# A RWKV/conv/Fourier/MoE backbone on one core: GpSimd's elementwise work in the attention units goes to VectorE, a broadcast copy to TensorE

## Chip, cores and metric

One core of a Trainium2 chip runs one program, the whole two-layer block. The metric is the device time of one execution in microseconds (us); the median of three runs of the kernel before is 3627.87 us (3625.42 to 3634.18).

## The reference, cut to what matters

1280 tokens (256 of context, 1024 latent) of width 1024 go through two layers. Each layer projects the normed tokens to 2944 columns; half of the model is a bidirectional RWKV-7 time mixing with 8 heads of 64:

```python
w_log = -softplus(-(decay_w0 + tanh(lw) @ decay_w2)) - 0.5
decay = exp(-exp(w_log))
a = sigmoid(iclr_a0 + la @ iclr_a2)
kk = normalised(k * k_k)
k_dir = k * (1.0 + (a - 1.0) * k_a)
s = s * d_t - (s @ kk_t)(kk_t * a_t)^T + v_t k_t^T
y = sum over directions of s r_t;  bonus = sum(r * k_dirs[dn] * r_k) * v
```

The rest of a layer (a gated short convolution, a Fourier mix, an output projection, a mixture of 32 experts) is not touched by the change.

## The kernel before, in words

The recurrence is computed in chunks of C = 64 tokens, of which there are 20. For each layer the work ahead of the sequential scan is cut into 16 units (L818). A unit is a pair of heads p (head e = 0 on partitions 0 to 63, e = 1 on 64 to 127), a half hf of the tokens (640 tokens, 10 chunks) and a direction d. The units run in pairs that share p and hf. Beside them runs the input projection (L386): 128x512 fp32r matmuls that a pacing object places on TensorE between the matmuls of the units, a fixed share per unit (L838). The program's order of each engine comes from a scheduler with its own timeline of the engines; SyncE (SP) issues nearly all DMAs from one queue in program order.

What one unit does:

- `gates` (L492): two matmul groups make the logits; ScalarE takes tanh of half of them, and VectorE maps each by 0.5x + 0.5 to a sigmoid (L508) for the decays `sg` and for `aa` (the a of the reference). VectorE's prefix scan over `sg` (L510) and two exponentials give E and Ei.
- `heads` (L477), once per pair of units: GpSimd copies the inverse norms `inv` out over 64 columns per head (L480), five matmuls with the identity transpose them (L484), and VectorE multiplies them with k (L485) to the normalised `kk`.
- `factors` (L517): ScalarE makes 1 + (a - 1) k_a from `aa` and VectorE multiplies it with k to `kd` (L523, L524). `aa` is multiplied by Ei (L526). `bk` holds, for each chunk, 128 columns: the keys kd Ei and the beta kk aa. VectorE fills the lower 64 partitions (L534, L535), GpSimd the upper 64 (L532, L533); the two heads have the two blocks in opposite order. VectorE makes `ar` (L536 to L542). In every second unit GpSimd adds the `kd` of the two directions and multiplies the sum with r (L544, L545), and a DMA writes it to prD (L546).
- `attn` (L549): matmuls of `bk` with `ar` (L561), masked by VectorE into X (L566), DMAs of `ar` and X (L573 to L578), then, in two groups, five TensorE transposes of `bk` (L583), copied by ScalarE (L587) and stored (L589).
- `inverse` (L591): for three units at a time GpSimd inverts 120 triangular 32x32 blocks by 60 small operations (L605, L607); ScalarE transposes them and DMAs store them (L612, L622). It reads the blocks that `attn` wrote to gD (L600).
- `merge` (L625): loads the blocks of one unit again (L635, L636) into the single buffer `zt` and makes 64x64 inverses by small matmuls (L645, L647), copied by ScalarE and stored (L655). The merge of unit u - 6 is loaded at unit u.

`bk`, `ar`, `aa` and `kd`'s sum have one buffer (or two for `kd`), so a unit waits for the readers of the one before. The loop that orders it all:

```python
g = gates(p, hf, d, *lw)
if prev is not None:
    attn(*prev)
if u % 2 == 0:
    kk, kds = heads(p, hf, rks[p][1], invs[p]), []
prev = (p, hf, d) + factors(p, hf, d, *rks[p], kk, g, kds)
```

Of the kernel before, what the change touches and what calls it, by code (L numbers as in the profile page):

```python
# [9 lines left out]
F32 = mybir.dt.float32  # L10
# [3 lines left out]
AF = mybir.ActivationFunctionType  # L14
OP = mybir.AluOpType
# [4 lines left out]
P = 128  # L20
# [11 lines left out]
C = 64  # L32
# [15 lines left out]
HT, HC = T // 2, NCH // 2  # L48
# [75 lines left out]
class K:  # L124
# [223 lines left out]
    def inproj(self, l, last):  # L348
        nc, tc, a = self.nc, self.tc, self.a
# [5 lines left out]
        sp = tc.alloc_tile_pool(name="ip", bufs=1, reuse_waits="tile")  # L355
        un = tc.alloc_tile_pool(name="un", bufs=1, side="right", reuse_waits="tile")
# [3 lines left out]
        pace = Pace(tc)  # L360
        om = sp.tile([P, 15], F32, name="om")
        nc.vector.tensor_scalar(om, self.vec("mu", 0, 15), -1.0, 1.0, op0=OP.mult, op1=OP.add)
        oka = sp.tile([P, 4], F32, name="oka")
        nc.vector.tensor_scalar(oka, self.vec("ka", 0, 4), -1.0, 1.0, op0=OP.mult, op1=OP.add)
        wah = sp.tile([P, 2, 8], F32, name="wah")
        nc.vector.tensor_scalar(wah[:, 0], self.vec("w0", 0, 8), 0.5, None, op0=OP.mult)
        nc.vector.tensor_scalar(wah[:, 1], self.vec("a0", 0, 8), 0.5, None, op0=OP.mult)
# [15 lines left out]
        def bank():  # L383
            return bk_[0].tile([P, 1024], F32, name="ps1", bufs=bk_[1])
# [91 lines left out]

        def heads(p, hf, k, inv):  # L477

            kk = un.tile([P, HT], F32, name="kk", bufs=2)
            nc.gpsimd.tensor_copy(kk.rearrange("q (t e d) -> q t e d", e=2, d=64),  # L480
                                 inv[:, 5 * hf:5 * hf + 5, :, None].to_broadcast([P, 5, 2, 64]))
            ps = bank()
            for t in range(5):
                nc.tensor.matmul(ps[:, t * P:(t + 1) * P], kk[:, t * P:(t + 1) * P], self.ident, start=True, stop=True)  # L484
            nc.vector.scalar_tensor_tensor(kk, k[:, hf * HT:(hf + 1) * HT], self.vec("kk", p), ps[:, :HT],  # L485
                                           op0=OP.mult, op1=OP.mult)
            return kk.rearrange("q (c t) -> q c t", t=C)
# [4 lines left out]
        def gates(p, hf, d, lw, la):  # L492


            t0 = hf * HT
            hs = slice(64 * d, 64 * d + 64)
            sg = un.tile([P, HC, C], F32, name="sg")
            aa = un.tile([P, HC, C], F32, name="aa")
            for i, (w, src, dst) in enumerate(((w2, lw, sg), (a2, la, aa))):
                ps = bank().rearrange("q (h t) -> q h t", h=2)[:, :, :320]  # L500
                for q in range(2):
                    mm = nc.tensor.matmul(ps[:, q], w[hs, p * P:(p + 1) * P],
                                          src[hs, t0 + 320 * q:t0 + 320 * (q + 1)], start=True, stop=True)
                pace.point(mm, W_GATE[i])

                nc.scalar.activation(flat(dst).rearrange("q (h t) -> q h t", h=2), ps, AF.Tanh,
                                     bias=wah[:, i, 4 * d + p:4 * d + p + 1], scale=0.5)
                nc.vector.tensor_scalar(dst, dst, 0.5, 0.5, op0=OP.mult, op1=OP.add)  # L508
            rev = slice(None, None, -1) if d else slice(None)
            nc.vector.tensor_tensor_scan(flat(sg)[:, rev], rst, flat(sg)[:, rev], 0.0, op0=OP.mult, op1=OP.add)  # L510
            E = un.tile([P, HC, C], F32, name="E")
            Ei = un.tile([P, HC, C], F32, name="Ei")
            nc.scalar.activation(E, sg, AF.Exp, scale=-CC)
            nc.scalar.activation(Ei, sg, AF.Exp, scale=CC)
            return aa, E, Ei

        def factors(p, hf, d, r, k, kk, g, kds):  # L517
            aa, E, Ei = g
            rev = slice(None, None, -1) if d else slice(None)
            e0 = 0 if d else C - 1  # L520
            nc.vector.tensor_copy(self.wc[d][:, p, hf * HC:(hf + 1) * HC], E[:, :, e0])
            kd = un.tile([P, HC, C], F32, name="kd", bufs=2)
            nc.scalar.activation(kd, aa, AF.Identity, bias=oka[:, p:p + 1], scale=self.vec("ka", p))  # L523
            nc.vector.tensor_tensor(kd, kd, cv(k, hf), op=OP.mult)  # L524
            kds.append(kd)
            nc.vector.tensor_tensor(aa, aa, Ei, op=OP.mult)  # L526


            ar = un.tile([P, 2, HC, C], F32, name="ar")
            bk = un.tile([P, HC, 2, C], F32, name="bk")  # L530
            lo, hi = slice(0, 64), slice(64, 128)
            nc.gpsimd.tensor_tensor(bk[hi, :, 0, :], kd[hi], Ei[hi], op=OP.mult)  # L532
            nc.gpsimd.tensor_tensor(bk[hi, :, 1, :], kk[hi, :, rev], aa[hi, :, rev], op=OP.mult)  # L533
            nc.vector.tensor_tensor(bk[lo, :, 1, :], kd[lo], Ei[lo], op=OP.mult)  # L534
            nc.vector.tensor_tensor(bk[lo, :, 0, :], kk[lo, :, rev], aa[lo, :, rev], op=OP.mult)  # L535
            if d == 0:  # L536
                nc.vector.tensor_tensor(ar[:, 0, :, 1:], kk[:, :, 1:], E[:, :, :C - 1], op=OP.mult)
                nc.vector.tensor_copy(ar[:, 0, :, 0:1], kk[:, :, 0:1])
            else:
                nc.vector.tensor_tensor(ar[:, 0, :, 1:], kk[:, :, C - 2::-1], E[:, :, :0:-1], op=OP.mult)  # L540
                nc.vector.tensor_copy(ar[:, 0, :, 0:1], kk[:, :, C - 1:C])
            nc.vector.tensor_tensor(ar[:, 1], cv(r, hf), E, op=OP.mult)  # L542
            if len(kds) == 2:
                nc.gpsimd.tensor_tensor(kds[0], kds[0], kds[1], op=OP.add)  # L544
                nc.gpsimd.tensor_tensor(kds[0], kds[0], cv(r, hf), op=OP.mult)  # L545
                nc.sync.dma_start(self.prD[p][:, hf * HT:(hf + 1) * HT], flat(kds[0]))  # L546
            return ar, bk

        def attn(p, hf, d, ar, bk):  # L549

            GR = ((0, 5), (5, 5))
            half = lambda e: slice(64 * e, 64 * e + 64)
            img = slice(hf * HC, (hf + 1) * HC)

            Xs = [un.tile([P, 2, HC, C], F32, name="X", bufs=2) for _ in range(2)]
            for c0, n in ((0, 4), (4, 3), (7, 3)):
                ps = bank().rearrange("q (e c s t) -> q e c s t", e=2, s=2, t=C)
                for c in range(n):
                    for e in range(2):
                        h = half(e)  # L560
                        mm = nc.tensor.matmul(ps[:, e, c], bk[h, c0 + c].rearrange("q s t -> q (s t)"), ar[h, :, c0 + c, :],  # L561
                                              start=True, stop=True)
                pace.point(mm, W_ATTN)
                for e in range(2):
                    mv = msk[:, d, e].rearrange("q (s t) -> q s t", s=2)
                    nc.vector.tensor_tensor(Xs[e][:, :, c0:c0 + n].rearrange("q s c t -> q c s t"), ps[:, e, :n],  # L566
                                            mv[:, None].to_broadcast([P, n, 2, C]), op=OP.mult)
            for e in range(2):
                h, o = half(e), half(1 - e)
                X = Xs[e]  # L570
                sn = "q s (n c) t -> q (s n) (c t)"
                for v, rows in ((ar[h], h), (X[o], o)):
                    nc.sync.dma_start(self.rlD[d][e][img, rows, p, :].rearrange("m q x -> q m x"),  # L573
                                      v.rearrange(sn, c=2))
                nc.sync.dma_start(self.abD[d][hf * 5:hf * 5 + 5, h, 1, p, :].rearrange("n q x -> q n x"),
                                  X[h, 1].rearrange("q (n c) t -> q n (c t)", c=2))
                m = (2 * place[p, hf, d] + e) * HC
                nc.sync.dma_start(self.mats(self.gD, m, HC), X[h, 0])  # L578

            for c0, n in GR:  # L580
                ps = bank()
                for c in range(n):
                    mm = nc.tensor.transpose(ps[:, c * P:(c + 1) * P], bk[:, c0 + c].rearrange("q s t -> q (s t)"),  # L583
                                             self.ident)
                pace.point(mm, W_ATTN)
                bt = un.tile([P, 5, P], F32, name="bt", bufs=2)
                nc.scalar.activation(bt[:, :n].rearrange("q c t -> q (c t)"), ps[:, :n * P], AF.Copy)  # L587
                ch = slice(hf * HC + c0, hf * HC + c0 + n)
                nc.sync.dma_start(self.btD[d][ch, :, p, :].rearrange("c q x -> q c x"), bt[:, :n])  # L589

# [1351 lines left out]
```

## Time and profile before

| what | us |
|---|---|
| median of 3 runs (lowest, highest) | 3627.87 (3625.42, 3634.18) |
| the profiled execution | 3623.64 |
| its span, first to last instruction | 3621.7 |
| TensorE busy in the span | 3063.4 |
| VectorE busy | 2281.6 |
| ScalarE busy | 1880.5 |
| GpSimd busy | 1178.0 |

The profiled execution took 3623.64 us, 1.9 us more than its span. The units of the first layer run from about 170 to 600 us of the span, those of the second from about 2000 to 2430 us. Engines are named PE (TensorE matmuls), PEld (its weight loads), DVE (VectorE), ACT (ScalarE), POOL (GpSimd) and SPq (SyncE's queue). A name such as `bk<-kd,Ei` is the tile written and the tiles read; an idle time is put down to what ended it.

### The profile page before, as it was taken

Reading aid. Unit: us, or ns where it says so; the run is one execution under the profiler, and the core shown is the slowest. Engines: PE = TensorE matmul, PEld = TensorE weight load, DVE = VectorE, ACT = ScalarE, POOL = GpSimd, SP = SyncE. Lnnn points to the kernel's source line nnn. Section 1 sums busy time; section 2 is a strip of 40 time slices with the busy share of each in tenths; the row PEclk is TensorE's granted clock in tenths of the full one; section 3 lists DMA queues with packets and bytes.
Section 4 is the critical chain, followed back from the end, with each engine's and each line's share of the span. In section 5 each row is a group of like instructions: output and inputs, shape, how many; then the busy total and the mean of one; then the engine's idle time right before and its main releaser. Section 6 shows DMA issues by size and latency. Waiting matters only on the chain. (4 is left out here: it accounts for less than half of the span.)

```text
span 3621.7 us, 59282 instructions
## 1 busy us (share of the span) xinstructions
PE 3063.4 (85%) x22308; PEld 2426.6 (67%) x22308; DVE 2281.6 (63%) x3543; ACT 1880.5 (52%) x2838; POOL 1178.0 (33%) x1101
## 2 busy tenths in 40 slices
PE   6998788888997999999829988778878978999992
PEld 3776666676686777777616766556666857777772
DVE  4265566134487888888672665652334778888886
ACT  4343433335344777778652434323343467777783
POOL 0037675211221222222140276743113122233323
PEclk8998888899998999999959988778988989999996
DMA  6677888879746899999667578889795488899995
GB/s 241 207 167 173 185 192 181 246 230 315 260 142 243 334 339 338 365 373 363 257 227 258 144 169 181 176 180 252 240 285 167 133 315 317 331 366 364 360 366 205
DMA packets 708060, 922.35 MB, mean 255 GB/s; under 512 B 335074, under 2 KB 561259, under 8 KB 657852
## 3 DMA queue, kind: packets, MB, share of 16 engines
q1 hardware_dynamic: 669456, 871.05, 75.8%
q0 software_dynamic: 38304, 47.49, 3.9%
q8 instruction: 177, 2.90, 0.3%
q14 instruction: 111, 0.91, 0.1%
q10 hardware_dynamic: 12, 0.00, 0.0%
HBM read 726.92 MB, written 203.23 MB: 257 GB/s over the span
## 5 line engine op out<-in xcount | busy, mean ns | idle before, releaser
L176 DVE TENSOR_TENSOR hl<-ld,hl 128x1024 fp32r<-128x1024 f32 x734 | 869.2, 1228 | 54.2 <-ACT hl L175 44.2
L175 ACT ACTIVATE hl<-ld 128x1024 fp32r<-128x1024 f32 x796 | 798.5, 1052 | 38.4 <-PE pR L1571 21.9
L1571 PE MATMUL pR<-hl,wk 128*128 128x512 f32 x1560 | 455.1, 400 | 0.0
L1571 PE MATMUL pU<-hl,wk 128*128 128x512 f32 x1560 | 446.9, 395 | 0.0
L397 PE MATMUL pb<-hh,wh 128*128 128x512 f32 (+1 forms) x1000 | 393.0, 394 | 10.2 <-ACT wh L175 5.4
L397 PE MATMUL pb<-hl,wh 128*128 128x512 f32 (+1 forms) x1000 | 389.1, 390 | 0.0
L397 PE MATMUL pb<-hh,wl 128*128 128x512 f32 (+1 forms) x1000 | 385.4, 386 | 0.0
L1595 PE MATMUL pA<-hl,wk 128*128 128x512 f32 x1560 | 382.9, 401 | 0.5 <-ACT wk L175 0.5
L1571 PEld LDWEIGHTS pU<-hl,wk 128*128 128x128 f32 x1560 | 294.5, 189 | 68.3
L1595 PEld LDWEIGHTS pA<-hl,wk 128*128 128x128 f32 x1560 | 292.7, 191 | 64.0 <-ACT wk L175 0.7
L1571 PEld LDWEIGHTS pR<-hl,wk 128*128 128x128 f32 x1560 | 288.3, 189 | 60.7 <-ACT wk L175 0.3
L176 POOL TENSOR_TENSOR hl<-ld,hl 128x1024 fp32r<-128x1024 f32 x62 | 184.2, 2971 | 422.4 <-ACT hl L175 422.4
L397 PEld LDWEIGHTS pb<-hh,wh 128*128 128x128 f32 x1000 | 200.2, 200 | 76.8 <-issue 14.1
L1602 POOL DMA_INDIRECT yb<-wk,sca x64 | 94.8, 1482 | 468.2 <-ACT wk L1601 452.1
L1276 PE MATMUL pA<-hl,wk 128*128 128x512 f32 x864 | 226.6, 413 | 7.7 <-POOL wk L176 4.0
L397 PEld LDWEIGHTS pb<-hl,wh 128*128 128x128 f32 x1000 | 201.1, 201 | 37.9 <-issue 10.3
L397 PEld LDWEIGHTS pb<-hh,wl 128*128 128x128 f32 x1000 | 200.2, 200 | 35.2 <-issue 4.6
L1100 POOL DMA_DIRECT2D yD<-yt x72 | 58.0, 805 | 433.7 <-ACT yt L1099 391.6
L1276 PEld LDWEIGHTS pA<-hl,wk 128*128 128x128 f32 x864 | 163.0, 195 | 49.2 <-issue 6.0
L1088 DVE TENSOR_TENSOR tm<-pR,ST 128x256 f32<-128x256 f32 x76 | 32.1, 423 | 249.4 <-PE pR L1083 237.4
L175 ACT ACTIVATE wk<-pm 128x256 fp32r<-128x256 f32 (+1 forms) x195 | 88.8, 455 | 185.6 <-PE pm L1586 169.3
L607 POOL TENSOR_TENSOR gt<-gt,tmp 120x30 f32<-120x30 f32 (+14 forms) x240 | 168.3, 701 | 17.7
(425 smaller groups left out, 5389.6 us busy)
## 6 DMA issues: line engine op xcount, KB each, us to landing
ld<-in_exp_gu SPq DMA_DIRECT2D x260, 1024.0 KB
ld<-in_exp_dn SPq DMA_DIRECT2D x130, 1024.0 KB
st<-rlD SPq DMA_DIRECT2D x80, 512.0 KB
wr<-in_w_in SPq DMA_DIRECT2D x46, 512.0 KB
rlD<-ar SPq DMA_DIRECT2D x64, 320.0 KB
rlD<-X SPq DMA_DIRECT2D x64, 320.0 KB
btD<-bt SPq DMA_DIRECT2D x64, 320.0 KB
st<-abD SPq DMA_DIRECT2D x40, 512.0 KB
```

Of the source, the lines that this page charges most:

```text
L175: nc.scalar.activation(hi, src, AF.Copy)
L176: (eng or nc.vector).tensor_tensor(lo, src, hi.bitcast(F32), op=OP.subtract)
L397: mm = nc.tensor.matmul(ps[:, :n], w[:, k, :], h[:, k, c0:c0 + n], start=(k == 0 and i == 0), stop=(k == KD - 1 and i == 2))
L607: eng.tensor_tensor(gt[:, 0:j, j + 1:32], gt[:, 0:j, j + 1:32], tv, op=OP.add)
L1088: nc.vector.tensor_tensor(tm, RS[:, 1], ST[d], op=OP.add)
L1100: nc.gpsimd.dma_start(self.yD[d][:, ch * C:(ch + 1) * C, :], yt.rearrange("q p d -> q (p d)"))
L1276: nc.tensor.matmul(ps, oo[o][:, k, :], w[k][w_][:, fs], start=(k == 0 and q == 0), stop=(k == KD - 1 and q == 2))
L1571: nc.tensor.matmul(o, x.xT[xi][:, kk, :], w[wi][:, k, :], start=(kk == 0 and i == 0), stop=(kk == KD - 1 and i == 2))
L1595: nc.tensor.matmul(x.y[n], x.h[:, hi_, f, :], dw[wi][:, 0, n * 512:(n + 1) * 512], start=(f == 0 and i == 0), stop=(f == 3 and i == 2))
L1602: nc.gpsimd.indirect_dma_start(out=yb, out_offset=bass.IndirectOffsetOnAxis(ap=x.sca, axis=0), in_=o, in_offset=None, bounds_check=2 * T - ...
```

## The change

GpSimd keeps only the block inverses in the units.

- `heads`: the copy on GpSimd goes. The matmuls take `inv` itself, broadcast, as weights: ten with 64 output rows (two per token tile) in place of five with 128. `kk` has one buffer in place of two.
- `gates`: the map 0.5x + 0.5 of `sg` goes from VectorE to ScalarE; that of `aa` goes away. It is folded into the constants of `kd` (`hka`, `oka`), into L526 (now (aa + 1) Ei) and into beta (factor 0.5).
- `factors`: `bk` has three blocks per chunk. The middle one is beta for both heads, one VectorE instruction on 128 partitions; head 0 has its keys in block 2, head 1 in block 0, one VectorE instruction on 64 partitions each. The sum of the `kd` and its product with r go to VectorE.
- `attn`: the weights of head e are blocks 1 and 2, or 0 and 1. The five TensorE transposes of a group become ten matmuls of 64 rows with the identity's 64x64 corner, and the copy (L587) reads PSUM in another order.

```diff
@@ -360,8 +360,11 @@
         pace = Pace(tc)
         om = sp.tile([P, 15], F32, name="om")
         nc.vector.tensor_scalar(om, self.vec("mu", 0, 15), -1.0, 1.0, op0=OP.mult, op1=OP.add)
+
+        hka = sp.tile([P, 4], F32, name="hka")
+        nc.vector.tensor_scalar(hka, self.vec("ka", 0, 4), 0.5, None, op0=OP.mult)
         oka = sp.tile([P, 4], F32, name="oka")
-        nc.vector.tensor_scalar(oka, self.vec("ka", 0, 4), -1.0, 1.0, op0=OP.mult, op1=OP.add)
+        nc.vector.tensor_scalar(oka, self.vec("ka", 0, 4), -0.5, 1.0, op0=OP.mult, op1=OP.add)
         wah = sp.tile([P, 2, 8], F32, name="wah")
         nc.vector.tensor_scalar(wah[:, 0], self.vec("w0", 0, 8), 0.5, None, op0=OP.mult)
         nc.vector.tensor_scalar(wah[:, 1], self.vec("a0", 0, 8), 0.5, None, op0=OP.mult)
@@ -476,12 +479,12 @@
 
         def heads(p, hf, k, inv):
 
-            kk = un.tile([P, HT], F32, name="kk", bufs=2)
-            nc.gpsimd.tensor_copy(kk.rearrange("q (t e d) -> q t e d", e=2, d=64),
-                                 inv[:, 5 * hf:5 * hf + 5, :, None].to_broadcast([P, 5, 2, 64]))
+            kk = un.tile([P, HT], F32, name="kk")
             ps = bank()
             for t in range(5):
-                nc.tensor.matmul(ps[:, t * P:(t + 1) * P], kk[:, t * P:(t + 1) * P], self.ident, start=True, stop=True)
+                for e in range(2):
+                    nc.tensor.matmul(ps[64 * e:64 * e + 64, t * P:(t + 1) * P],
+                                     inv[:, 5 * hf + t, e:e + 1].to_broadcast([P, 64]), self.ident, start=True, stop=True)
             nc.vector.scalar_tensor_tensor(kk, k[:, hf * HT:(hf + 1) * HT], self.vec("kk", p), ps[:, :HT],
                                            op0=OP.mult, op1=OP.mult)
             return kk.rearrange("q (c t) -> q c t", t=C)
@@ -505,7 +508,8 @@
 
                 nc.scalar.activation(flat(dst).rearrange("q (h t) -> q h t", h=2), ps, AF.Tanh,
                                      bias=wah[:, i, 4 * d + p:4 * d + p + 1], scale=0.5)
-                nc.vector.tensor_scalar(dst, dst, 0.5, 0.5, op0=OP.mult, op1=OP.add)
+                if i == 0:
+                    nc.scalar.activation(dst, dst, AF.Copy, bias=0.5, scale=0.5)
             rev = slice(None, None, -1) if d else slice(None)
             nc.vector.tensor_tensor_scan(flat(sg)[:, rev], rst, flat(sg)[:, rev], 0.0, op0=OP.mult, op1=OP.add)
             E = un.tile([P, HC, C], F32, name="E")
@@ -520,19 +524,18 @@
             e0 = 0 if d else C - 1
             nc.vector.tensor_copy(self.wc[d][:, p, hf * HC:(hf + 1) * HC], E[:, :, e0])
             kd = un.tile([P, HC, C], F32, name="kd", bufs=2)
-            nc.scalar.activation(kd, aa, AF.Identity, bias=oka[:, p:p + 1], scale=self.vec("ka", p))
+            nc.scalar.activation(kd, aa, AF.Identity, bias=oka[:, p:p + 1], scale=hka[:, p:p + 1])
             nc.vector.tensor_tensor(kd, kd, cv(k, hf), op=OP.mult)
             kds.append(kd)
-            nc.vector.tensor_tensor(aa, aa, Ei, op=OP.mult)
+            nc.vector.scalar_tensor_tensor(aa, aa, 1.0, Ei, op0=OP.add, op1=OP.mult)
 
 
             ar = un.tile([P, 2, HC, C], F32, name="ar")
-            bk = un.tile([P, HC, 2, C], F32, name="bk")
-            lo, hi = slice(0, 64), slice(64, 128)
-            nc.gpsimd.tensor_tensor(bk[hi, :, 0, :], kd[hi], Ei[hi], op=OP.mult)
-            nc.gpsimd.tensor_tensor(bk[hi, :, 1, :], kk[hi, :, rev], aa[hi, :, rev], op=OP.mult)
-            nc.vector.tensor_tensor(bk[lo, :, 1, :], kd[lo], Ei[lo], op=OP.mult)
-            nc.vector.tensor_tensor(bk[lo, :, 0, :], kk[lo, :, rev], aa[lo, :, rev], op=OP.mult)
+            bk = un.tile([P, HC, 3, C], F32, name="bk")
+            for e in range(2):
+                h = slice(64 * e, 64 * e + 64)
+                nc.vector.tensor_tensor(bk[h, :, 2 - 2 * e], kd[h], Ei[h], op=OP.mult)
+            nc.vector.scalar_tensor_tensor(bk[:, :, 1], kk[:, :, rev], 0.5, aa[:, :, rev], op0=OP.mult, op1=OP.mult)
             if d == 0:
                 nc.vector.tensor_tensor(ar[:, 0, :, 1:], kk[:, :, 1:], E[:, :, :C - 1], op=OP.mult)
                 nc.vector.tensor_copy(ar[:, 0, :, 0:1], kk[:, :, 0:1])
@@ -541,8 +544,8 @@
                 nc.vector.tensor_copy(ar[:, 0, :, 0:1], kk[:, :, C - 1:C])
             nc.vector.tensor_tensor(ar[:, 1], cv(r, hf), E, op=OP.mult)
             if len(kds) == 2:
-                nc.gpsimd.tensor_tensor(kds[0], kds[0], kds[1], op=OP.add)
-                nc.gpsimd.tensor_tensor(kds[0], kds[0], cv(r, hf), op=OP.mult)
+                nc.vector.tensor_tensor(kds[0], kds[0], kds[1], op=OP.add)
+                nc.vector.tensor_tensor(kds[0], kds[0], cv(r, hf), op=OP.mult)
                 nc.sync.dma_start(self.prD[p][:, hf * HT:(hf + 1) * HT], flat(kds[0]))
             return ar, bk
 
@@ -550,6 +553,8 @@
 
             GR = ((0, 5), (5, 5))
             half = lambda e: slice(64 * e, 64 * e + 64)
+
+            left = lambda e, c: bk[half(e), c, 1 - e:3 - e].rearrange("q s t -> q (s t)")
             img = slice(hf * HC, (hf + 1) * HC)
 
             Xs = [un.tile([P, 2, HC, C], F32, name="X", bufs=2) for _ in range(2)]
@@ -558,7 +563,7 @@
                 for c in range(n):
                     for e in range(2):
                         h = half(e)
-                        mm = nc.tensor.matmul(ps[:, e, c], bk[h, c0 + c].rearrange("q s t -> q (s t)"), ar[h, :, c0 + c, :],
+                        mm = nc.tensor.matmul(ps[:, e, c], left(e, c0 + c), ar[h, :, c0 + c, :],
                                               start=True, stop=True)
                 pace.point(mm, W_ATTN)
                 for e in range(2):
@@ -578,13 +583,15 @@
                 nc.sync.dma_start(self.mats(self.gD, m, HC), X[h, 0])
 
             for c0, n in GR:
-                ps = bank()
+                ps = bank().rearrange("q (e c d) -> q e c d", e=2, d=C)
                 for c in range(n):
-                    mm = nc.tensor.transpose(ps[:, c * P:(c + 1) * P], bk[:, c0 + c].rearrange("q s t -> q (s t)"),
-                                             self.ident)
+                    for e in range(2):
+                        h = half(e)
+                        mm = nc.tensor.matmul(ps[:, e, c], left(e, c0 + c), self.ident[h, h], start=True, stop=True)
                 pace.point(mm, W_ATTN)
                 bt = un.tile([P, 5, P], F32, name="bt", bufs=2)
-                nc.scalar.activation(bt[:, :n].rearrange("q c t -> q (c t)"), ps[:, :n * P], AF.Copy)
+                nc.scalar.activation(bt[:, :n].rearrange("q c (e d) -> q c e d", e=2),
+                                     ps[:, :, :n].rearrange("q e c d -> q c e d"), AF.Copy)
                 ch = slice(hf * HC + c0, hf * HC + c0 + n)
                 nc.sync.dma_start(self.btD[d][ch, :, p, :].rearrange("c q x -> q c x"), bt[:, :n])
```

## Rows read from the trace of the kernel before

**Rows 1.** Stretches: us, busy PE, PEld, DVE, ACT, POOL (count), TensorE clock, DMA share, GB/s.

```profile
160.00:280.00 120.00, 117.36 (x722) 93.04 (x721) 78.66 (x101) 53.31 (x71) 37.35 (x33) 0.99 0.65 153
280.00:600.00 320.00, 271.55 (x2180) 217.85 (x2179) 193.36 (x260) 121.42 (x172) 224.15 (x269) 0.87 0.86 184
1990.00:2110.00 120.00, 118.53 (x709) 90.77 (x708) 76.34 (x101) 51.58 (x70) 39.85 (x36) 0.99 0.67 160
2110.00:2430.00 320.00, 254.20 (x1947) 197.22 (x1946) 186.70 (x248) 112.88 (x164) 220.37 (x269) 0.80 0.82 175
```

**Rows 2.** TensorE's waits, 170 to 640 us: us in total, times, longest.

```profile
PE pq L645 <- DMA zt<-xD: 30.8, 8, 13.4
PE ps L561 <- POOL bk L533: 7.6, 3, 3.7
```

**Rows 3.** TensorE's waits, 2000 to 2470 us.

```profile
PE pq L645 <- DMA zt<-xD: 25.8, 10, 6.7
PE ps L561 <- POOL bk L533: 14.3, 4, 5.8
```

**Rows 4.** SyncE's waits, 170 to 640 us.

```profile
SPq L546 <- POOL kd L545: 15.8, 4, 6.4
SPq L612 <- POOL gt L607: 11.2, 3, 4.2
```

**Rows 5.** SyncE's waits, 2000 to 2470 us.

```profile
SPq L546 <- POOL kd L545: 30.9, 7, 10.8
SPq L612 <- POOL gt L607: 7.7, 2, 4.6
```

**Rows 6.** Timeline near 396 us: start, us, engine, line, idle before.

```profile
395.00 1.53 POOL L533 TENSOR_TENSOR bk<-kk,aa 64x640 f32<-64x640 f32 x1
396.56 0.79 ACT L506 ACTIVATE aa<-ps,wah 128x640 f32<-128x640 f32 x1 [4.40 <-POOL bk L533]
```

**Rows 7.** GpSimd, 170 to 640 us: groups, count, busy us, mean ns, idle before.

```profile
L533 POOL TENSOR_TENSOR bk<-kk,aa 64x640 f32<-64x640 f32 x16 | 34.1, 2133 | 2.8 <-DVE kk L485 2.5
L532 POOL TENSOR_TENSOR bk<-kd,Ei 64x640 f32<-64x640 f32 x16 | 32.3, 2016 | 43.6 <-PE ps L583 20.9 <-issue 17.2 <-ACT v L430 3.6
L544 POOL TENSOR_TENSOR kd<-kd 128x640 f32<-128x640 f32 x8 | 15.0, 1869 | 25.8 <-DVE kd L524 15.5 <-issue 10.3
L545 POOL TENSOR_TENSOR kd<-kd,r 128x640 f32<-128x640 f32 x8 | 12.5, 1559 | 0.2
```

**Rows 8.** Timeline of TensorE near 333, 338, 506 and 763 us (the scan).

```profile
332.82 0.71 PE L583 MATMUL ps<-ident,bk 128*128 128x128 f32 x5
...
333.29 0.48 PE L397 MATMUL pb<-hh,wl 128*128 128x512 f32 x1
...
333.84 1.28 PE L484 MATMUL ps<-ident,kk 128*128 128x128 f32 x10
...
338.31 0.19 PEld L397 LDWEIGHTS pb<-hh,wh 128*128 128x128 f32 x1 [0.44 <-issue]
...
506.44 1.83 PE L561 MATMUL ps<-ar,bk 64*128 64x128 f32 x28 [0.76 <-ACT sg L506]
...
508.21 0.50 PE L397 MATMUL pb<-hl,wh 128*128 128x512 f32 x1
...
762.68 0.69 PE L1061 MATMUL pR<-st,st 128*64 128x64 f32 x16
```

**Rows 9.** Instruction groups on VectorE, 170 to 640 us.

```profile
L535 DVE TENSOR_TENSOR bk<-kk,aa 64x640 f32<-64x640 f32 x16 | 23.9, 1494 | 0.2
L534 DVE TENSOR_TENSOR bk<-kd,Ei 64x640 f32<-64x640 f32 x16 | 19.3, 1207 | 21.9 <-PE ps L583 21.7
L542 DVE TENSOR_TENSOR ar<-r,E 128x640 f32<-128x640 f32 x16 | 14.0, 874 | 3.1 <-DMA rlD<-ar 3.1
L508 DVE TENSOR_SCALAR sg<-sg 128x640 f32<-128x640 f32 x16 | 10.9, 682 | 27.4 <-ACT sg L506 27.4
```

**Rows 10.** Instruction groups on ScalarE, 170 to 640 us.

```profile
L513 ACT ACTIVATE E<-sg 128x640 f32<-128x640 f32 x16 | 11.7, 734 | 15.5 <-DVE sg L510 15.4
```

## The prediction

> **What bounds the kernel now.** I read the table of stretches first [rows 1]. Each layer's units fall into two parts. While units 0 to 3 run (160 to 280 us, 1990 to 2110 us) TensorE is busy 117.36 and 118.53 of 120 us at a granted clock of 0.99: it is the bound there, by the projection that runs beside the units. In the later units it is busy 271.55 and 254.20 of 320 us, so 48.5 and 65.8 us idle, 114 us together, and the clock falls to 0.87 and 0.80 (a mean of its two levels, 2.4 and 1.2 GHz). Nobody is full there: VectorE 193 of 320, ScalarE 121, GpSimd 224, the DMA engines 0.86 and 0.82. It is bound by waits in the loop of unit, inverse, DMA and merge.
>
> TensorE's waits come next. The largest is for the merge's loads of `zt`, 30.8 us in the first layer and 25.8 in the second; direct waits for GpSimd's beta (L533) are 7.6 and 14.3 us [rows 2, 3]. What makes the loads late is read from SyncE's queue, which is in order: it stands 15.8 and 30.9 us before the store to prD (L546) until GpSimd has made the product (L545), and 11.2 and 7.7 us before the store of the inverses (L612) until GpSimd has ended them, 65.6 us together [rows 4, 5]. Behind each of these stand X, `btD` and the loads of `zt`. The timeline shows why GpSimd is late: L533 is queued between the small operations of an inverse, starts at 395.00 us, and ScalarE, which may not overwrite `aa` before that, sat 4.40 us and starts at 396.56 [rows 6]. So the unit that is due waits for an inverse that is wanted three units later.
>
> **The change part by part.**
>
> GpSimd loses L532, L533, L544 and L545: 32.3 + 34.1 + 15.0 + 12.5 = 93.9 us per layer [rows 7], and the copy of L480. Its inverses are then one uninterrupted run each. Who waited for it in the unit now waits for VectorE.
>
> TensorE gets dearer. A group of five transposes takes 0.47 us (332.82 to the next projection at 333.29). Its ten matmuls with the identity are fp32 and become two instructions each, as the ten instructions of L484 for five matmuls show, so 20 instructions on a 64x128 part of the array. No row shows that shape with 64 columns. The nearest is L561, the same weights with 128 columns: 28 in 1.83 us, 65 ns each; the other end is L1061 in the scan, 16 in 0.69 us, 43 ns [rows 8]. I take 65 ns, since the weights are of the same size: 1.31 us per group, 0.84 more, and 1.68 us more per unit; by 43 ns it is 0.8 us per unit. `heads` goes from 10 instructions in 1.28 us to 20 of 64 output rows: between 43 and 128 ns each (L1061, L484), 0.9 to 2.6 us; at 65 ns it is 1.30 us, no change. All 32 units: 54 us at the full clock.
>
> Here the Trainium skill, "TensorEngine Tiling (Array Packing)", section Key Properties, speaks against the change: it says that a change of tiling mode drains the engine. The trace agrees in one place: after L502 (64 rows) the next weight load shows 0.44 us idle; it does not after L561, where the next projection starts at 508.21, before the group's modelled end at 508.27 [rows 8]. By the rule each of the two groups would cost another 0.44 us, 28 us over 32 units; the sum takes none of it.
>
> VectorE: out go L534 and L535 (1.21 and 1.49 us) and two tensor_scalars of about 0.68 (L508), 4.1 us per unit. In come two key products on 64 partitions (1.21 each at L534's mean), one beta on 128 partitions (0.87, as L542, which has the same 640 columns) and, as two per pair, 0.87 us for the `kd` sum: 4.2 us [rows 9]. L526 keeps its length but for a second operation. No change within 0.1 us; if the durations lengthen as L535 does beside GpSimd, 1.5 us more, which its idle 127 of 320 us cover [rows 1]. Without that cover X would come later and SyncE with it. The three products that end `bk` come to 2.4 to 3.3 us on one engine, where GpSimd alone needed 4.1 (L532 and L533 at their means, more where an inverse stands between).
>
> ScalarE: one more pass per unit, 0.73 us as the exponential of the same shape [rows 10], in place of a VectorE step of 0.68 on the same chain. The map of `aa` leaves the chain without substitute. Two ends: 0.73 us more or 0.7 us less per unit; I take zero, since one stands for one and ScalarE is idle 199 of 320 us. The changed reading order of L587 and the constants at the head of a layer go at nothing: same elements, and four columns. `bk`'s third block and `kk`'s lost buffer move no wait that I can find, as VectorE now writes and reads `kk` alone, in order.
>
> SyncE's DMAs are the same in number and size. The store to prD is now ready when VectorE's last product ends, and it stands ahead of X in the queue as before. If VectorE takes the product up late, the wait of [rows 4, 5] returns under another name.
>
> **The sum**, against the profiled execution (3623.6 us; 4.3 us below the median of the runs):
> - Units 0 to 3 of both layers: 8 x 1.68 = 13 us more, fully exposed.
> - Stalls that end: all of the 7.6 + 14.3 us that TensorE waits for L533, and a third of SyncE's 65.6 us, because the rest of its queue and the DMA engines are nearly as late: 22 + 22 = 44 us less. The ends are 22 and 88 us.
> - The clock: at 0.87 and 0.80 of full speed TensorE's busy time holds 0.13 x 271.55 + 0.20 x 254.20 = 86 us of lost clock beside 114 us of idle, 0.75 us each. Half of that for the stalls that end: 0.38 x 44 = 17 us less; the ends are 0 and 33.
> - Added matmuls in the later 24 units: 24 x 1.68 = 40 us, 48 at a clock of 0.84. About 70 us of idle remain; I hide half: 24 us more. The ends are 0 and 48.
> 13 - 44 - 17 + 24 = -24 us: 3600 for the profiled execution, 3604 beside the median.
>
> **The rivals.**
> 1. *The next wait takes over (no change).* The inverse still passes SyncE, the DMA engines are at 0.86, and `zt` has one buffer, so its loads go on being late. Then only the 22 us of direct waits end, with 8 of clock, against 13 + 24: +7, and between 3617 and 3639. For it speaks that 56.6 us of TensorE's waits name a DMA, only 21.9 GpSimd. Against it: SyncE itself names GpSimd for 65.6 us.
> 2. *TensorE becomes the bound (slower).* The place is the two groups of L583 and `heads`. If all 32 units show 1.68 us, at the later clock 13 + 48, and `heads` its upper price (1.3 us x 16 pairs = 21), and 22 + 8 come back: +52, 3680; without the dear `heads` 3659. It decides once the added 40 us of the later units find less than about 20 us of idle that nothing else needs. For it speaks that TensorE is the busiest engine in every stretch; against it, that it idles 114 us. The rule on drains would add up to 28 us here.
> 3. *The loop closes fully (much faster).* Two thirds of SyncE's wait return, 22 + 44 with 25 of clock, and the added matmuls hide but for 5 us: 13 - 66 - 25 + 5 = -73, 3555.
> That GpSimd is not relieved at all is excluded by the diff: nothing of it but the inverses is left in the units.
>
> **How the numbers follow.** What a measurement of this kernel can tell from no change is 0.3%, 11 us. My forecast has 0.46 and covers 3575 to 3616; rival 3 has 0.10, rival 1 0.23, rival 2 0.21. Faster: 0.46 + 0.10 and a little of rival 1, 0.57; same 0.23; slower 0.20. The predicted time is that of the likeliest case, 3604 us. Its own range is 3575 to 3616. The range for 8 in 10 takes in rival 1 and the near parts of 2 and 3: 3560 to 3648.
>
> **What would show it.** Right: no wait for GpSimd at L561, L506 and L546; TensorE's idle in the later units down from 114 us by some 40, L583 as 40 instructions per unit at about 65 ns, units 0 to 3 longer by about 7 us per layer, VectorE's sum there unchanged. Wrong: SyncE's L546 waiting as long for VectorE; L583's instructions over 80 ns or with idle time before the next projection; the clock no higher; VectorE's instructions as long as before and X later. The forecast fails above all if the idle that GpSimd leaves is taken by `zt`'s loads, or if the added matmuls stand where TensorE has no idle time.

## The result, and the profile after

The changed kernel takes 3757.13 us in the median of four executions (3753.96 to 3768.58) against 3626.64 us before (3623.01 to 3634.18): a ratio of 1.0363, 95% interval 1.0335 to 1.0390. The forecast was 3604 us with a range to 3648; it missed by sign and by range.

The intended part happened. GpSimd's busy time fell from 1178 us to this:

The profile of the changed kernel, busy time of the engines (us, share of the span, instructions):

```profile
PE 3147.7 (84%) x23428; PEld 2490.6 (66%) x23428; DVE 2249.4 (60%) x3545; ACT 1902.2 (51%) x2870; POOL 988.3 (26%) x989
```

VectorE, which took over GpSimd's products, is no busier (2281.6 before), ScalarE has 22 us more. TensorE has 84 us more. The time is lost in the stretch of the units. To compare the kernels over the same units, the next tables run from the first unit's prefix scan to the fourth's and from there to the last unit's, in each layer. The first stretch holds the transposes (L583, L590 in the changed kernel) of two units, the second those of twelve. First the kernel before, over these stretches:

```profile
178.70:239.60 60.90, 58.39 (x368) 47.65 (x367) 41.92 (x55) 28.36 (x39) 17.13 (x9) 1.00 0.64 150
239.60:545.80 306.20, 262.03 (x2006) 208.32 (x2007) 187.87 (x230) 119.94 (x170) 212.17 (x250) 0.87 0.85 184
2009.40:2067.40 58.00, 58.00 (x355) 45.44 (x355) 43.20 (x60) 28.61 (x39) 16.73 (x9) 1.00 0.65 153
2067.40:2367.10 299.70, 247.84 (x1770) 191.08 (x1770) 184.34 (x228) 112.48 (x158) 200.47 (x226) 0.84 0.80 175
```

Then the changed kernel (columns as in [rows 1]: length, then busy time of PE, PEld, DVE, ACT, POOL, granted clock, DMA share, GB/s):

```profile
178.20:252.10 73.90, 67.43 (x446) 53.77 (x444) 39.13 (x55) 31.86 (x44) 0.00 (x0) 0.89 0.58 139
252.10:621.70 369.60, 292.87 (x2523) 235.76 (x2523) 173.99 (x229) 128.82 (x188) 164.98 (x244) 0.83 0.70 154
2100.80:2173.50 72.70, 67.07 (x462) 52.54 (x456) 41.57 (x59) 31.60 (x44) 0.00 (x0) 0.98 0.58 141
2173.50:2530.90 357.40, 284.65 (x2347) 214.86 (x2343) 174.81 (x229) 125.59 (x179) 159.70 (x235) 0.78 0.72 156
```

The four stretches are 149 us longer together; beside the change, they differ by the share of the projection that falls into them (1510 matmuls in the changed kernel, 1462 before). VectorE and GpSimd work less than before in the later units, ScalarE 9 to 13 us more in a longer stretch, and the DMA engines fall from 0.85 and 0.80 to 0.70 and 0.72: no engine is full there. TensorE's idle time in the later units goes from 96 us (44.2 + 51.9) to 149 (76.7 + 72.8), and its clock falls. In SyncE's queue the wait that grew most is the one for the inverses. These rows answer to [rows 4, 5], first layer (170 to 715 us), then second (2100 to 2630 us):

```profile
SPq L619 <- POOL gt L614: 38.0, 3, 13.3
SPq L662 <- ACT zt L661: 30.3, 7, 7.0
SPq L578 <- DVE X L571: 26.4, 9, 9.1
...
SPq L619 <- POOL gt L614: 58.6, 4, 22.7
SPq L682 <- ACT bt L680: 17.9, 6, 6.9
```

L619 is the store of the inverses (L612 before), for which SyncE stood 11.2 and 7.7 us before. GpSimd's inverses are indeed uninterrupted, some 46 us each from the first to the last instruction where they were about 60, and yet SyncE waits five times as long for them. The timeline of SyncE around the second inverse of the first layer shows why:

```profile
384.55 0.60 SPq L642 DMA_DIRECT2D zt<-gD  x1
...
393.88 1.64 SPq L583 DMA_DIRECT2D gD<-X  x1
...
409.18 0.38 SPq L662 DMA_DIRECT2D abD<-zt  x1
422.97 0.34 SPq L619 DMA_DIRECT2D gD<-gt  x1
423.42 4.02 SPq L642 DMA_DIRECT2D zt<-gD  x1
...
434.11 1.68 SPq L583 DMA_DIRECT2D gD<-X  x1
435.89 0.70 SPq L596 DMA_DIRECT2D btD<-bt  x1
...
455.55 0.36 SPq L662 DMA_DIRECT2D abD<-zt  x1
...
461.49 0.34 SPq L629 DMA_DIRECT2D xD<-zt  x1
...
478.02 0.57 SPq L607 DMA_DIRECT2D gt<-gD  x1
```

After the merge's store at 409.18 SyncE issues nothing until the inverse ends at 422.9 us. Behind the store (422.97) stand the loads of the next merge into `zt` (423.42) and a whole unit's X stores. Since `zt` has one buffer, ScalarE may copy the finished inverse into it only when that merge has stored (455.55), and the next load of `gt` is issued at 478.02.

From this standstill the way to TensorE leads through `btD`: its store (435.89) is late too, behind the merge's loads and X; ScalarE may fill that buffer of `bt` again only when it is done, and TensorE waits for ScalarE:

```profile
439.89 0.60 ACT L680 ACTIVATE bt<-pl 128x512 f32<-128x512 f32 x1 [19.99 <-DMA btD<-bt]
440.55 1.11 PE L677 MATMUL pl<-ident,v 128*128 128x128 f32 x4 [18.31 <-ACT bt L680]
```

TensorE's waits that name ScalarE's `bt` are 82 us in the changed kernel (both layers, as above) against 8 before; those for the merge's loads of `zt`, the largest before, fell from 56.6 to 45.5 us.

GpSimd stands idle after each inverse, as its timeline shows at the start of the second, third and fourth inverse (L608):

```profile
376.13 0.16 POOL L608 MEMSET gt<- 120x32 f32 x1 [45.23 <-DMA gt<-gD]
484.18 0.15 POOL L608 MEMSET gt<- 120x32 f32 x1 [61.23 <-DMA gt<-gD]
577.62 0.15 POOL L608 MEMSET gt<- 120x32 f32 x1 [45.40 <-DMA gt<-gD]
```

In the kernel before, the store stands behind one more unit's X stores and behind the merge's loads. The scheduler, which makes the order of each queue from a timeline of its own, had made another order for the changed kernel. Below, the six pauses of GpSimd between the end of an inverse and the start of the next (three in each layer) serve as a measure: 157 us in the kernel before, in which products of GpSimd lie too (as in numbers 2 and 6 below), and 307 us after.

### The profile page after: what moved, and what is told of

The parts are those of the page before. It is cut to its first block, busy times and chain, and to the rows that moved or that the text cites. A ratio compares the mean times of both kernels' runs of the same rounds, so it can differ in the third digit from the quotient of the medians.

```text
span 3766.7 us, 61362 instructions
## 1 busy us (share of the span) xinstructions
PE 3147.7 (84%) x23428; PEld 2490.6 (66%) x23428; DVE 2249.4 (60%) x3545; ACT 1902.2 (51%) x2870; POOL 988.3 (26%) x989
## 5 line engine op out<-in xcount | busy, mean ns | idle before, releaser
L400 PE MATMUL pb<-hh,wh 128*128 128x512 f32 (+1 forms) x1000 | 401.9, 403 | 6.0 <-ACT k L433 3.5
L400 PE MATMUL pb<-hl,wh 128*128 128x512 f32 (+1 forms) x1000 | 396.9, 397 | 0.0
L400 PE MATMUL pb<-hh,wl 128*128 128x512 f32 (+1 forms) x1000 | 394.2, 396 | 0.0
```

The source lines that it names most:

```text
L400: mm = nc.tensor.matmul(ps[:, :n], w[:, k, :], h[:, k, c0:c0 + n], start=(k == 0 and i == 0), stop=(k == KD - 1 and i == 2))
```

## Experiments

Two theories stood at the start. **Order**: SyncE's queue was put together for a GpSimd that is done sooner, and the early store holds up the loop. **TensorE**: the 30 added instructions per unit are the loss. Line numbers are those of each kernel; helpers shift them by up to 16.

| kernel | us | ratio to before [95%] | six pauses of GpSimd, us |
|---|---|---|---|
| changed | 3757 | 1.0363 [1.0335, 1.0390] | 307 |
| 1 store held back | 3713 | 1.0214 [1.0190, 1.0238] | 269 |
| 2 products with the identity alone | 3727 | 1.0256 [1.0232, 1.0280] | 244 |
| 3 GpSimd's products on VectorE alone | 3626 | 0.9973 [0.9953, 0.9993] | 191 |
| 4 changed, stores on other queues | 3691 | 1.0160 [1.0128, 1.0192] | 250 |
| 5 as 3, stores on other queues | 3586 | 0.9871 [0.9847, 0.9895] | 182 |
| 6 transposes three times over | 3692 | 1.0166 [1.0139, 1.0193] | 207 |
| 7 changed, transposes of halves | 3580 | 0.9861 [0.9838, 0.9883] | 194 |
| 8 as 7, stores on other queues | 3597 | 0.9910 [0.9889, 0.9932] | 197 |
| 9 changed, all queues in the order of 7 | 3619 | 0.9971 [0.9955, 0.9987] | 191 |
| 10 as 7, all queues in the order of changed | 3767 | 1.0381 [1.0364, 1.0398] | 305 |
| 11 changed, TensorE's queue as 7 | 3764 | 1.0372 [1.0344, 1.0401] | 296 |
| 12 changed, the other four queues as 7 | 3653 | 1.0059 [1.0036, 1.0083] | 213 |
| 13 changed, SyncE's queue as 7 | 3678 | 1.0133 [1.0107, 1.0159] | 251 |
| 14 changed, ScalarE's and VectorE's as 7 | 3734 | 1.0295 [1.0268, 1.0321] | 300 |

**1. The store held back.** An ordering edge on SyncE's queue, no wait; `mark` is the last DMA of `attn` or `merge` traced before this unit:

```diff
-                    inverting()
+                    with tc.issue_after(mark):
+                        inverting()
```

> The changed kernel, with one ordering rule added: the finish of an inverse (store of gD from gt, ScalarE's copy, store of xD) may be issued only behind the DMAs of the unit before, so that SyncE's queue again has two units' X stores between the load of gt and its store, as the kernel before has. Nothing else differs; the arithmetic is that of the changed kernel. Order theory (SyncE stands before a store that was queued one unit too early, 38 + 59 us, and what is behind it comes late): the store's wait falls below 25 us over both layers and at least 60 us of the 133 us come back, so at most 3695 us. TensorE theory (the 40 added instructions per unit are the loss): at least 3740 us.

3713 us: neither theory's number. SyncE's wait for the store fell from 97 to 37 us (25.4 + 11.7), but only 44 us came back. The edge did only a part of what was meant: two of the first layer's stores (414.75 and 522.18 us) now stand behind the next merge's loads, but still have one unit's X stores between load and store, not two. The merge and `zt` stayed where they were, and GpSimd's pauses shrank by 38 us only.

**2. The products with the identity alone.** The kernel before with

```diff
-                    mm = nc.tensor.transpose(ps[:, c * P:(c + 1) * P], bk[:, c0 + c]..., self.ident)
+                    for e in range(2):
+                        mm = nc.tensor.matmul(ps[:, e, c], left(e, c0 + c), self.ident[h, h], start=True, stop=True)
```

> The kernel before, with beta's three blocks, the products with the identity in place of the transposes (40 instructions per unit in place of 10) and one buffer of kk; GpSimd keeps its four products, ScalarE and VectorE keep theirs. Only TensorE's added work is in it. TensorE theory: 90 us or more above the kernel before, 3715 us or more. Order theory: the added work is paid where TensorE is full (13 us) and in part of the later units, so 3640 to 3670 us.

As in the change, `bk` has three blocks and `kk` one buffer, so the edit is not TensorE's work alone. 3727 us, as the TensorE theory had it. Taken alone it would have settled the case for the wrong theory.

**3. GpSimd's products on VectorE alone.** The kernel before with `nc.vector` for `nc.gpsimd` in four lines.

> The kernel before, with the four products of GpSimd (L532, L533, L544, L545) on VectorE, each with the same operands and the same partitions; the transposes stay. GpSimd is relieved, TensorE has no added work, and SyncE's queue has the order of the kernel before (two units' X stores between load and store of an inverse). Order theory: with that order the relief of GpSimd brings something, or at worst VectorE's two added products (about 3.5 us per unit) eat it: 3590 to 3640 us. TensorE theory: the same, since TensorE has nothing added. A third theory (VectorE is what is late once it makes all of beta) gives over 3680 us.

3626 us, 0.3% below before. Relieving GpSimd is worth little by this edit alone, and VectorE is not late.

**4. The stores off SyncE's queue.** The changed kernel with

```diff
-                    nc.sync.dma_start(self.diag(self.gD, j0, n), gt)
+                    nc.gpsimd.dma_start(self.diag(self.gD, j0, n), gt)
...
-                nc.sync.dma_start(self.diag(self.xD, j0, n), xt)
+                nc.scalar.dma_start(self.diag(self.xD, j0, n), xt)
```

> The changed kernel, with the store of gD from gt issued by GpSimd, right behind the inverse, and the store of xD by ScalarE, right behind its copy; SyncE has neither. Order theory: SyncE no longer stands at the store, so at most 3720 us; but the merge's loads keep their early place in its queue and take over part of the wait, so not as fast as with the order restored. TensorE theory: at least 3740 us.

3691 us: 66 us come back without a change to TensorE's work. The order theory holds for that much.

**5 and 6. The same stores with experiment 3, and the transposes of the kernel before made three times.**

```diff
-                for c in range(n):
+                for c in list(range(n)) * 3:
                     mm = nc.tensor.transpose(
```

> The kernel before with GpSimd's four products on VectorE and, besides, the store of gD issued by GpSimd and the store of xD by ScalarE. TensorE has nothing added and SyncE stands before neither store. Order theory: those waits are short in the kernel before (11.2 + 7.7 us), so little is to be had: 3585 to 3620 us. If GpSimd's relief was worth what the prediction gave it and only the order of the stores held it back, 3570 us or less.

> The kernel before with every group of five transposes made three times over into the same bank (the last one counts): 10 more instructions of 128x128 per group, 0.94 us at 0.47 us per five, 60 us over 32 units at the full clock, the same TensorE time as the added products with the identity, but on the whole array. TensorE theory, if any added TensorE time is paid 1.5 times: 3700 to 3740 us. If instead the products on half of the array cost more than their time (a lower clock behind them), the whole array is cheaper: at most 3680 us.

Number 5 is 1.3% faster than before, at the lower edge of what was expected. Number 6 lies between the two expectations: 61 us more than the kernel before beside it (3631 us) for 60 us of added TensorE work, where number 2 lost 92 (against 3635) for less. So the loss of number 2 was more than TensorE's time; which part of the rest is its order and which `kk`'s one buffer was not tried.

**7 and 8. Transposes of halves.** The changed kernel with one word of the change taken back:

```diff
-                        mm = nc.tensor.matmul(ps[:, e, c], left(e, c0 + c), self.ident[h, h], start=True, stop=True)
+                        mm = nc.tensor.transpose(ps[:, e, c], left(e, c0 + c), self.ident[h, h])
```

> The changed kernel with a transpose of each half of beta in place of the product with the identity: one instruction in place of two, 20 per unit in place of 40, all else as changed. By the 65 ns of one instruction about 0.65 us per group in place of 1.26. TensorE theory: half of the added work goes, and about 45 us or more with it: 3690 to 3720 us. If TensorE's work is not the point: 3740 us or more.

> The same transposes of halves, and the two stores on GpSimd's and ScalarE's queues. If TensorE's work and SyncE's stand at the store are the two causes and add up: 65 us below the kernel with the halves alone, 3625 to 3655 us, about the kernel before.

3580 us, 177 us below the changed kernel and 1.4% below before: far outside what either theory gave. TensorE's added work is some 54 us at the full clock, so 177 cannot be its time. And moving the stores, which had helped twice, made this kernel 17 us slower. The effects do not add up, as they would if each were a price of its own. What differs besides is the order: with the transposes the scheduler puts the store behind two units' X stores, as in the kernel before, although the inverses are as short as in the changed kernel. So the first form of the order theory, that the shorter inverses had moved the store, fell as well: one word, the form of the matmuls, makes the difference.

**9 and 10. The two orders exchanged.** Both kernels trace the same instructions one for one. For each engine, edges that order without a wait put the instructions of the units into the order that the scheduler made for the other kernel (`mine` are the engine's instructions as traced, `steps` leads through them in the other order):

```diff
+        for s in steps:
+            at += s
+            if prev is not None:
+                tc.add_manual_dep(mine[at], prev.name, ..., reason="order")
+            prev = mine[at]
```

> The changed kernel, instruction for instruction, but in the units each engine's queue is put by edges into the order that the scheduler made for the kernel with transposes of halves. The products with the identity stay (40 instructions per unit). If the order is what costs: the kernel with transposes of halves (3580 us) plus the added TensorE time of 32 units (54 us at the full clock) and no more, 3620 to 3655 us. If the products themselves cost three times their time on the chip whatever the order: 3720 us or more.

> The other way round: the kernel with transposes of halves, each engine's queue in the units put by edges into the order that the scheduler made for the changed kernel. TensorE has 20 instructions per unit. If the order is what costs: 3680 us or more, 100 us above the same kernel in its own order. If the products are what costs: at most 3610 us.

This decides it. The changed kernel, instruction for instruction, takes 3619 us in the other order; the fast kernel takes 3767 us in the changed kernel's. The order is worth 138 us one way and 187 the other. TensorE's added instructions cost 40 us in the good order (3619 - 3580) and nothing in the bad one (3757 against 3767), where TensorE idles 149 us in the later units. SyncE's timeline of number 9 around the same inverse (L635 is the store, L658 and L659 the merge's loads, L623 the load of `gt`):

```profile
383.48 1.59 SPq L599 DMA_DIRECT2D gD<-X  x1
393.24 1.36 SPq L635 DMA_DIRECT2D gD<-gt  x1
404.30 0.41 SPq L678 DMA_DIRECT2D abD<-zt  x1
409.24 0.34 SPq L645 DMA_DIRECT2D xD<-zt  x1
...
421.09 1.09 SPq L658 DMA_DIRECT2D zt<-gD  x1
...
424.70 0.41 SPq L623 DMA_DIRECT2D gt<-gD  x1
```

The inverse ends at 391.6 us; the next load of `gt` is issued 33 us later, not 55. The merge that is stored at 404.30 was loaded from 375.01 on, before the store, so `zt` is free sooner. TensorE's waits that name ScalarE's `bt` are down to 14 us. Its stretches, to be read against those of before and after:

```profile
177.20:242.00 64.80, 64.80 (x463) 52.86 (x461) 39.08 (x55) 32.60 (x45) 0.00 (x0) 1.00 0.68 160
242.00:538.90 296.90, 269.76 (x2446) 215.56 (x2445) 174.51 (x229) 126.03 (x182) 155.88 (x225) 0.90 0.86 187
2028.20:2094.50 66.30, 66.30 (x444) 51.48 (x437) 42.03 (x59) 31.90 (x44) 0.00 (x0) 0.97 0.67 164
2094.50:2384.50 290.00, 258.64 (x2323) 197.70 (x2322) 172.78 (x228) 123.83 (x176) 151.90 (x225) 0.90 0.86 189
```

**11 to 14. Which queue.** The same edges for some of the engines alone; the scheduler makes the queues without edges anew each time, so these four shares are no clean prices.

> The changed kernel with TensorE's queue alone, in the units, in the order of the kernel with transposes of halves; the other queues as the scheduler then makes them. There the store of gD from gt still stands early in SyncE's queue (one unit's X stores, not two, between load and store). If TensorE's order (how the projection stands among the units' matmuls) is what costs: 3620 to 3660 us. If SyncE's early store is what costs: 3700 us or more.

> The changed kernel with the queues of SyncE, ScalarE, VectorE and GpSimd in the order of the kernel with transposes of halves, and TensorE's as the scheduler then makes it, which differs from that. The store stands as before. If SyncE's early store is what costs: 3620 to 3660 us. If TensorE's order is what costs: 3690 us or more.

> The changed kernel with SyncE's queue alone, in the units, in the order of the kernel with transposes of halves; the four compute engines' queues as the scheduler then makes them. If SyncE's order is what cost the 105 us that the four queues together gave back: 3650 to 3680 us, and from the end of an inverse to the next load of gt about 26 us as there, not 44. If it is the order of ScalarE and VectorE: 3720 us or more.

> The changed kernel with ScalarE's and VectorE's queues, in the units, in the order of the kernel with transposes of halves; SyncE's and TensorE's as the scheduler then makes them, with the store of gD early in SyncE's queue. If SyncE's order is what costs: 3720 us or more. If it is the order of ScalarE and VectorE: 3650 to 3690 us.

TensorE's queue alone brings nothing (3764 us), the four others 104 us (3653). Of these SyncE's alone brings 79 us (3678) and has no wait for the inverse's store left in the units; the time is just within its expected range, but from the end of an inverse to the next load pass 34 us, not 26, which leaves something to the other queues. ScalarE's and VectorE's bring 23 (3734); in number 14 the waits of SyncE's queue show it before the store again, in the first and the second layer:

```profile
SPq L635 <- POOL gt L630: 46.8, 4, 19.6
SPq L635 <- POOL gt L630: 53.1, 4, 20.6
```

79 and 23 are 102 of the 104. The last 34 us come with TensorE's queue, but only once the others are right. GpSimd's pauses go with the time in these kernels, roughly: 307 us at 3757, 251 at 3678, 213 at 3653, 191 at 3619; but 296 at 3764, and 191 to 197 us stand beside all of 3580 to 3626.

## Why the prediction was wrong, point by point

- **The step that failed** is the paragraph on SyncE: "the same in number and size" is true, and from it the prediction took that the queue would keep its order, with the prD store the only entry whose wait was worked out. The queues' order, which the sum puts at nothing, was no constant of the kernel; the scheduler made it anew. The store of the inverses, whose wait of 11.2 and 7.7 us was counted among the stalls that end, grew to 38.0 and 58.6 us. Experiments 9 and 10 give the whole of the loss (131 us) to the order of the queues, 138 and 187 us; number 13 gives 79 us to SyncE's queue alone. The store to prD did as foretold: SyncE's wait before it fell from 46.7 to 14.6 us (6.4 + 8.2), and no wait of TensorE names GpSimd any more.
- **The sum for a kernel in the other order** came near, in part because two errors cancel; number 9 is its test. The term for the full stretch holds: from the first unit's scan to the sixth's, which takes in the transposes of four units in each layer as that term does, number 9 is 13 us longer (6.3 + 6.8; 13 predicted). First the kernel before, then number 9:

```profile
178.70:280.90 102.20, 99.56 (x626) 80.07 (x625) 73.05 (x94) 45.60 (x62) 36.80 (x32) 1.00 0.73 169
2009.40:2111.00 101.60, 100.13 (x608) 77.78 (x608) 72.75 (x98) 43.70 (x60) 38.40 (x35) 1.00 0.73 170
177.20:285.70 108.50, 107.60 (x798) 86.72 (x798) 67.16 (x93) 49.71 (x69) 16.48 (x26) 1.00 0.74 174
2028.20:2136.60 108.40, 108.40 (x758) 84.55 (x751) 68.62 (x95) 47.41 (x65) 13.29 (x23) 0.98 0.69 163
```

  The later units are read from the stretches behind the fourth scan, which hold 24 units' transposes as the sum's other terms do. Work at the full clock (clock x busy) rose from 436 to 476 us, 40 as predicted. Busy time that the clock costs, by (1 - clock) x busy, fell from 74 to 53 us, 21, where the sum has 17 less for the stalls and 8 more for the added work, 9 less in all. TensorE's idle time fell by 38 us, from 96.0 to 58.5, where the sum has 44 of stalls and 24 of added work hidden in idle time, 68 in all. 40 - 38 - 21 is the 19 us by which these stretches are shorter, where the sum has 37. So the gain in idle time was forecast 30 us too large and the clock's 12 too small; which of the two idle terms (the stalls that end, the half that hides) was off, these rows don't tell. The kernel took 3619 us, not 3604.
- **TensorE's price** was right. TensorE's timeline of the changed kernel at the full clock:

```profile
204.56 1.33 PE L590 MATMUL ps<-ident,bk 64*128 64x64 f32 x20
205.82 0.44 PE L677 MATMUL pl<-ident,v 128*128 128x128 f32 x2
```

  A group takes 1.26 us to the start of the next (204.56 to 205.82; 1.31 predicted). The Trainium skill says in "TensorEngine Tiling (Array Packing)", section Key Properties, that a change of tiling mode drains the engine. At the prediction's 0.44 us per group that would be 28 us in all. No run shows such a cost: the 1.26 us run to a matmul on the whole array and would hold it, as would the 0.46 us of number 7's group below. The row of 0.44 us [rows 8] is idle time of the weight loads alone: of the matmuls, L502's group starts at 337.04 with a modelled 1.34 us, and the next projection starts before its end, at 338.31, as after L561. In the changed kernel the weight loads show 0.44 us again behind a group of the gates (L505, at 303.49 us), and no such idle behind any group of L590 in the stretches above.
- **Rival 2** had the sign, for the wrong reason: in number 11 TensorE's instructions and their order in the units are those of number 9, and the time is 145 us longer. **Rival 1** named the place (the inverse still passes SyncE, and `zt` has one buffer), but let its wait only stay as it was, and looked for it in the loads of `zt`. TensorE's waits for those fell; its waits for `bt` grew (82 us against 8). The price went from 7 us to over 130.
- **The clock** up to the fourth scan fell to 0.89 in the first layer, where it was 1.00 before. TensorE's timeline shows 1.82 us of waiting for ScalarE's `bt`, and then the second group of gates (L505) at half the rate of the first (2.13 us to the next instruction, against 1.18); the granted clock is 1.00 to 215.47 us and 0.53 from there to 217.60, near the lower of its two levels (1.2 of 2.4 GHz):

```profile
213.47 0.66 PE L677 MATMUL pl<-ident,v 128*128 128x128 f32 x4 [1.82 <-ACT bt L680]
213.88 0.48 PE L400 MATMUL pb<-hh,wl 128*128 128x512 f32 x1
214.29 1.34 PE L505 MATMUL ps<-lw,w 64*128 64x320 f32 x4
215.47 2.20 PE L505 MATMUL ps<-la,a 64*128 64x320 f32 x4
```

  Number 9, with the same instructions, keeps 1.00 there. So the fall in this stretch belongs to the order, not to products on half of the array.
- **GpSimd's relief** brought 0.3% in number 3. Number 7, which has the whole change but the dearer products, is 51 us below the kernel before beside it (3631 us), where the sum's two gains, 44 and 17, come to 61. Each of these kernels has an order of its own, so neither is a clean price of the relief.

What stays open: why the scheduler orders the queues otherwise for the one form of matmul, and which single entry of ScalarE's and VectorE's queues is worth their 23 us. Neither was tried. Nor is it shown how the 131 us divide over the single entries of SyncE's queue. The best kernel found is number 7, with 3580 us.

## What to carry to other kernels

Where a scheduler makes the order of the queues, an edit has two effects: its price on its engine, and a new order for all the others. Compare the order of the in-order queues (the DMA queue first) of both kernels before pricing anything, and look for an entry that waits for a long job and now stands ahead of other loads and stores. To tell the two effects apart, exchange the orders of the two kernels; changing one part at a time does not do it, since each part brings an order of its own.

## What the runs showed that was not expected

A transpose of a 64x128 half costs half of one of 128x128. The group in number 7, at the full clock:

```profile
204.88 0.52 PE L590 MATMUL ps<-ident,bk 64*128 64x64 f32 x10
205.34 0.39 PE L400 MATMUL pb<-hl,wh 128*128 128x256 f32 x1
```

Ten take 0.46 us to the next instruction, as five of 128x128 did (0.47, [rows 8]), where the twenty instructions of the products with the identity take 1.26. The Trainium skill says in "Perfetto Trace Analysis", section Transposes, that a logical transpose should be a transpose and not a matmul; the runs agree, at 0.8 us per group. And the same edit, products or transposes, was worth 177 us with the orders that the scheduler made, 40 us in the good order and nothing in the bad one.
